# First experts' rows: seven tiles gathered ahead of the last choices, the last tile added by one-hot products

## The chip, the cores and the metric

The kernel runs on one core of one Trainium2 chip. The core has a matrix engine (PE, whose weight loads are shown apart as PEld), three elementwise engines (DVE, ACT, POOL), a queue engine that issues transfers (SP), and 16 DMA engines that every queue shares. The metric is the device time of one execution in microseconds (us). The trace comes from one profiled execution of the kernel; the time is the median of three others.

## The reference, cut to what matters

One layer on 1024 tokens of 1024 channels: a mixer, a residual, a second norm, and a mixture of experts. Only the last two matter here. A router picks one group of 4 and two of 8 experts in it for each token, so each token goes to 2 of 32 experts:

```
x1 = x + gate1 * mixer(...)                       # (1024, 1024)
h  = rmsnorm(x1) * (1 + scale2) + shift2
p_grp = softmax(h @ w_rg + b_rg);  g = argmax(p_grp)
le    = (h @ w_re + b_re)[group g]                # 8 logits
top_p, top_e = top_k(softmax(le), 2);  e = 8 g + top_e
w_tok = p_g * top_p / sum(top_p)
for each expert: rows = h[tokens of the expert]   # here blocks of up to 128 rows
    y = (silu(rows @ w_gate[e]) * (rows @ w_up[e])) @ w_down[e]
x = x1 + gate2 * sum over a token's two experts of w_tok * y
```

Each expert has 6 MB of weights, so that 192 MB are read in the expert stage.

## The kernel before

Tokens are handled in eight tiles of 128. The output projection of the mixer (loop at L1476) makes one tile `t` of `x1` at a time; `residual`, `second_norm` and `router` follow it. `second_norm` (L1169) writes the normed rows to `h2_d` in HBM through POOL's queue; for the last tile (`LT` = 7) the work is cut into halves of 512 channels (`residual`, `scale_half`, `norm_half`, `router_T`, `router` with `hf` 0 and 1), and ACT's queue writes its rows. `choose` (L1227) turns a tile's logits into one-hot choices `oh` and `oab`, a chain of some twenty small DVE instructions.

A token's place among an expert's rows is its rank: matmuls with a strictly triangular matrix of ones (`psr`). Experts 0 and 1 (`FIX` = 2) are always handled first; for them `key` (L1330) holds the place and `sel01` is a one-hot matrix token by place. `first_slots` (L1545) multiplies it with the token numbers in `Vc`, `index` makes an integer of them, and `gather` (L1618) fetches the rows from `h2_d` into `xgs[r]`, cleared beforehand by `clear_xg`. All other experts are ordered by their counts in `order_of_experts` (L1336, three steps divided by `yield`): counts `pst`/`cnt`, a ranking `ord` and `psord`, and the places `pos` of all tokens. `weigh` (L1276) makes the token weights; its first step ends with three exponentials on ACT.

A block of rows goes through `st_x` (eight transposes by PE into `tpx`, split into a high and a low part `tHLx` by an ACT cast and a DVE subtraction, plain copy `tFx`), `st_gu` (products with gate, `wi` 0, and up, `wi` 1), `st_act`, `st_h` and `st_down`. `st_sel` makes the one-hot matrix of a further block, `st_slots` its indices and its gather. The names in the trace end in no number: `tpx` at L1661 is that of blocks 0, 1 and other large ones, at L1677 that of small ones; the third block of the program (number 16) is the first small one.

Weights come in loads of 1 MB into six buffers `big`: two for the gate matrix, two for up, two for down of each expert, in the order of `add_pieces` (L1450). A load is two pieces. `W.split` cuts a piece into a high and a low part (`wh` by ACT, `wl` by DVE, L148), except the up and down pieces of block 0 and all of small blocks, which PE takes whole. A buffer is free when both of its pieces have been split or used, and only then SP, which issues the loads in order, goes on to the load that needs it.

Every engine carries out its own instructions in the order in which the program records them (`tc.manual_schedule`), with waits where one engine needs another's result. PSUM tiles of one bank come from the pool `mps`, which has four buffers:

```
mps = ctx.enter_context(tc.tile_pool(name="mps", bufs=4, space=PSUM))
zps = ctx.enter_context(tc.tile_pool(name="zps", bufs=2, space=PSUM))
e4p = tc.alloc_tile_pool(name="e4p", bufs=3, side="right")
```

`xr` (the input rows of a tile, later its normed rows) and `xg` share the three buffers of `e4p`.

Of the kernel before, what the change touches and what calls it, by code (L numbers as in the profile page):

```python
# [18 lines left out]
P = 128  # L19
# [23 lines left out]
def hybrid_layer_kernel(ctx: ExitStack, tc: tile.TileContext, x, c, w_ada, b_ada, g_norm1, w_in, b_if,  # L43
# [11 lines left out]
    def tt(o, a, b, op, eng=V):  # L55
        return eng.tensor_tensor(out=o, in0=a, in1=b, op=op)  # L56
# [1061 lines left out]
    def k3(ap):  # L1118
        return ap.rearrange("p (k q) -> p k q", q=P)
# [22 lines left out]
    def router(t, hfs=(0, 1)):  # L1142
        for hf in hfs:
            if hf == 0:
                rt[t][1] = mps.tile([P, 512], F32, tag="m", name=f"psl{t}")
            for k in range(4 * hf, 4 * hf + 4):
                mm(rt[t][1][:, 0:36], rt[t][0][:, k, :], wrs[:, k, :], k == 0, k == KT - 1)
        if 1 in hfs:
            stt(logits[:, t, :], rt[t][1][:, 0:36], r2s[t], br, OP.mult, OP.add)
# [74 lines left out]
    def cb(ap, n, m=NT):  # L1224
        return ap.unsqueeze(1).broadcast_to([P, m, n])
# [245 lines left out]
            add_pieces(units[i + 1][0], 1)  # L1471


    xrs[0] = load_xr(0)
    stt(A2, A2, 1.0, g2row, OP.add, OP.mult)
    for t in range(NT):  # L1476
        if t + 1 < NT:
            xrs[t + 1] = load_xr(t + 1)
        mH, mL = mHL[t][:, 0], mHL[t][:, 1]
        if t + 1 < NT:  # L1480
            mg_split(t + 1)
        if 1 <= t < 4:
# [12 lines left out]
        if t < NT - 1:  # L1495
            for k in range(KT):
                products(k, (0, 1))
                if k == 1 and t == NT - 2:
                    drain()
                if k == 2 and t > 0:  # L1500
                    router_T(t - 1)
                if k == 5 and t > 0:
                    router(t - 1)
                    if t == NT - 2:
                        for _ in choose(t - 1, t):
                            pass
            if t == 0:
                router_const()
            if t in (4, 5):
                a_, b_ = ((0, 3), (3, 5))[t - 4]  # L1510
                lat.extend((choose(a_, b_), weigh(a_, b_)))
            for _ in range(6):
                fill(0)
            for hf in range(2):
                residual(t, hf)
            second_norm(t)
        else:
            for k in range(KT):
                products(k, (0,))
                if k == 2:  # L1520
                    router_T(t - 1)
                if k == 5:
                    router(t - 1)
            for _ in choose(t - 1, t):
                pass
            residual(t, 0)
            scale_half(t, 0)
            po[t][1] = zps.tile([P, 2, 512], F32, tag="z", name=f"o{t}_1")[:, 0, :]
            for k in range(KT):
                products(k, (1,))  # L1530
                if k == 4:
                    router_T(t, (0,))
                if k == 6:
                    ranks_early()
                    set_key(slice(0, LT), psr[0][:, 0:LT])
                    S.copy(rank[:, 0:LT], psr[0][:, 0:LT])
            router(t, (0,))
    sel01 = uo.tile([P, FIX, NT, P], BF16, tag="ar", bufs=2, name="sel01")
    psf = {}

    def sel_into(r, sl):
        n = sl.stop - sl.start
        tt(sel01[:, r, sl], cb(iota, P)[:, sl], key[:, sl, r:r + 1].broadcast_to([P, n, P]), OP.is_equal)

    def first_slots(r, a, b):  # L1545
        if a == 0:
            psf[r] = mps.tile([P, 512], F32, tag="m", name=f"slf{r}")
        for t in range(a, b):
            mm(psf[r][:, 0:3], sel01[:, r, t, :], Vc[:, t, 0, 0:3], t == 0, t == NT - 1)

    for r in range(FIX):
        sel_into(r, slice(0, LT))
    yp.release()
    ex = tc.alloc_tile_pool(name="ex", bufs=1, side="left")
    hlR.add(uo, "u", 2, UB, 5)
# [2 lines left out]
    residual(LT, 1)  # L1558
    scale_half(LT, 1)
    mean_square(LT)  # L1560
    router_T(LT, (1,))
    for hf in range(2):
        norm_half(LT, hf)
    router(LT, (1,))
    first_slots(0, 0, LT)
    S.dma_start(h2_d[LT * P:, :], xrs.pop(LT))
# [5 lines left out]
    xgs = [e4(f"xg{i}") for i in range(3)]  # L1572

    def clear_xg(g_):
        S.activation(k3(g_), iota.unsqueeze(1).broadcast_to([P, KT, P]), AF.Copy, scale=0.0)

    for g_ in xgs[0:2]:
        clear_xg(g_)
    for _ in choose(LT, NT):
        pass  # L1580
    mm(psr[1][:, 0:NE], strib, oab[:, LT, :], False, True)
    set_key(slice(LT, NT), psr[1][:, 0:NE].unsqueeze(1))
    S.copy(rank[:, LT, :], psr[1][:, 0:NE])


# [2 lines left out]
    def on_all_rows(o, cols):  # L1588

        for hf in range(2):  # L1590
# [5 lines left out]
    def index(pool, o, ps, c_, name):  # L1596

        sv = pool.tile([P, 1], F32, tag="sv" + name, bufs=6, name=f"sv{name}")
        red(sv, ps[:, c_:c_ + 3], OP.add)
        ts(o, sv, -1.0, OP.add)  # L1600

    def slots(pool, sels, vals, nv, name, c_):

# [75 lines left out]
        return o  # L1679

    ONE = [f"x{b}" for b in WHOLE]
    HALVES = (slice(0, 64), slice(64, 128))

    def st_sel(b):
# [108 lines left out]
            else:  # L1793
                scatter(y, d["idx"])


    for r in range(FIX):
        sel_into(r, slice(LT, NT))
        first_slots(r, LT if r == 0 else 0, NT)
        idx = mo.tile([P, 1], I32, tag="fidx", name=f"fidx{r}")  # L1800
        index(mo, idx, psf[r], 0, f"f{r}")
        gather(xgs[r], idx)
        R[r] = dict(xg=xgs[r])
    def blocks_of(i):
        return units[i] if i < len(units) else []

    places_ = order_of_experts()
# [9 lines left out]
    next(rest)  # L1817
# [6 lines left out]
    W.split()  # L1824
    W.split()
    W.split()
    st_x(1)
    st_sel(0)
    st_gu(0, 1, 0, 4)
    for b in blocks_of(2):  # L1830
        st_slots(b)
    st_slots(0, False)
    if dbg and "key" in dbg:
        nc.sync.dma_start(dbg["key"].rearrange("(t p) n -> p t n", p=P), key)
# [268 lines left out]
```

## Time and profile before

| what | value |
|---|---|
| time, median of 3 (range) | 1400.29 us (1399.58 to 1401.25) |
| the profiled execution's own time | 1400.88 us |
| its span, first to last instruction | 1399.1 us |
| PE busy | 1296.0 us, 93% of the span |
| DVE, ACT, POOL busy | 968.9, 477.7, 230.1 us |
| moved by DMA | 337.50 MB, mean 241 GB/s |

A row of the timeline is read so: start in us from the span's start, duration in us, engine, line, operation, output tile <- input tiles, shape, how many instructions the row merges, and in brackets the idle time before it and what ended it. An f32 product of PE (both operands f32) stands in the trace as two MATMUL instructions, a product of split parts (fp32r) as one. PEclk is the share of full clock that PE was granted: 1.00 is 2.4 GHz, 0.50 is 1.2 GHz.

### The profile page before, as it was taken

The page shows a single profiled execution, that of the slowest core. Times are in us where ns is not written, and L with a number is a line of the kernel's source. Part 1 is how long each engine was busy: PE and PEld are TensorE (multiplying, and loading weights), DVE is VectorE, ACT ScalarE, POOL GpSimd, SP SyncE. Part 2 cuts the span into 40 slices and gives each one's busy share as a digit, 9 for nine tenths or more (in the row PEclk, how much of TensorE's full clock was granted, in tenths as well). Part 3 has the DMA queues.
Part 4 walks back from the last instruction along what each step waited for, and adds up shares of the span by engine and source line. Part 5 has one row for each costly group of instructions (what it writes and reads, how often), then busy time and mean ns, then how long its engine had stood idle before and what let it go on. Part 6 is the DMA issues. An engine that isn't in the chain of part 4 may idle for free. (4 is left out here: it accounts for less than half of the span.)

```text
span 1399.1 us, 17600 instructions
## 1 busy us (share of the span) xinstructions
PE 1296.0 (93%) x6619; PEld 965.0 (69%) x6619; DVE 968.9 (69%) x1402; ACT 477.7 (34%) x650; POOL 230.1 (16%) x230
## 2 busy tenths in 40 slices
PE   3799999999989999899999689999898999999997
PEld 3678998889878888687887555656464756564643
DVE  6969987889997752655547776367575968584636
ACT  5221112223612222621222323225353735353523
POOL 3400111002112220106232002111010211111002
PEclk9799999999999999999999799999999999999999
DMA  9433454323453443455431549899999999999996
GB/s 295 129 121 138 149 181 165 117 80 106 136 158 125 132 144 105 139 166 162 170 118 49 210 184 383 325 379 404 414 411 407 406 380 414 391 409 387 414 385 258
DMA packets 121304, 337.50 MB, mean 241 GB/s; under 512 B 12532, under 2 KB 74272, under 8 KB 96384
## 3 DMA queue, kind: packets, MB, share of 16 engines
q1 hardware_dynamic: 106064, 290.81, 55.7%
q0 software_dynamic: 14672, 43.94, 8.4%
q10 hardware_dynamic: 480, 1.59, 0.3%
q8 instruction: 53, 0.87, 0.2%
q14 instruction: 35, 0.29, 0.1%
HBM read 303.37 MB, written 41.98 MB: 247 GB/s over the span
## 5 line engine op out<-in xcount | busy, mean ns | idle before, releaser
L56 DVE TENSOR_TENSOR wl<-big,wh 128x1024 fp32r<-128x1024 f32 x184 | 224.1, 1255 | 93.3 <-ACT wh L150 92.1
L150 ACT CAST wh<-big 128x1024 fp32r<-128x1024 f32 x184 | 185.6, 1049 | 154.4 <-DMA big<-in_w_e_gate_dram 88.1
L67 PE MATMUL z<-hH,wh 128*128 128x512 f32 x512 | 169.1, 412 | 7.1 <-DVE hH L378 7.1
L67 PE MATMUL gu<-wh,tHLx 128*128 128x512 f32 x528 | 170.7, 404 | 2.1 <-ACT wh L150 1.3
L67 PE MATMUL z<-hL,wh 128*128 128x512 f32 x512 | 163.8, 401 | 0.2 <-POOL hL L56 0.2
L67 PE MATMUL z<-hH,wl 128*128 128x512 f32 x512 | 163.4, 401 | 0.0
L64 DVE SCALAR_TENSOR_TENSOR cacc<-u,vec,cacc 128x1024 f32<-128x1024 f32 x120 | 159.1, 1326 | 2.8
L67 PE MATMUL gu<-big,tFx 128*64 128x512 f32 (+1 forms) x528 | 125.0, 608 | 0.0
L67 PEld LDWEIGHTS z<-hH,wh 128*128 128x128 f32 x512 | 97.6, 195 | 28.8 <-issue 8.1
L67 PEld LDWEIGHTS gu<-wh,tHLx 128*128 128x128 f32 x528 | 97.3, 190 | 28.1 <-ACT wh L150 6.6
L67 PEld LDWEIGHTS z<-hL,wh 128*128 128x128 f32 x512 | 98.5, 192 | 24.9 <-POOL hL L56 0.7
L67 PEld LDWEIGHTS z<-hH,wl 128*128 128x128 f32 x512 | 98.5, 192 | 23.5
L67 PE MATMUL gu<-wl,tHLx 128*128 128x512 f32 x264 | 107.0, 405 | 7.2 <-DVE wl L56 6.9
L1624 POOL DMA_INDIRECT y_d<-ye,idx x24 | 37.7, 1569 | 330.0 <-DVE ye L64 307.3
L67 PEld LDWEIGHTS gu<-big,tFx 128*64 128x64 f32 (+1 forms) x528 | 38.4, 141 | 69.4 <-issue 67.9
L67 PE MATMUL zt<-wh,hH 128*128 128x256 f32 (+1 forms) x256 | 73.1, 286 | 0.0
L67 PE MATMUL o<-woH,mHL 128*128 128x512 f32 x256 | 72.8, 400 | 0.0
L67 PE MATMUL zt<-wh,hL 128*128 128x256 f32 (+1 forms) x256 | 72.8, 284 | 0.0
L67 PE MATMUL zt<-wl,hH 128*128 128x256 f32 (+1 forms) x256 | 72.2, 282 | 0.0
L67 PE MATMUL py<-wh,tHLh 128*128 128x512 f32 x256 | 71.6, 400 | 0.5 <-DVE tHLx L56 0.4
L67 PEld LDWEIGHTS gu<-wl,tHLx 128*128 128x128 f32 x264 | 50.0, 189 | 27.6 <-DVE wl L56 16.9
L56 DVE TENSOR_TENSOR wl<-raw,wh 128x1024 fp32r<-128x1024 f32 (+1 forms) x45 | 57.1, 1274 | 15.7 <-ACT wh L150 15.7
(418 smaller groups left out, 2101.8 us busy)
## 6 DMA issues: line engine op xcount, KB each, us to landing
big<-in_w_e_gate_dram SPq DMA_DIRECT2D x64, 1024.0 KB, 9.8
big<-in_w_e_up_dram SPq DMA_DIRECT2D x64, 1024.0 KB
big<-in_w_e_down_dram SPq DMA_DIRECT2D x64, 1024.0 KB, 8.7
raw<-in_w_in_dram SPq DMA_DIRECT2D x38, 512.0 KB, 4.1
ar<-in_w_ada_dram SPq DMA_DIRECT2D x16, 1024.0 KB, 6.6
araw<-in_w_ada_dram SPq DMA_DIRECT2D x8, 1024.0 KB, 9.6
y_d<-zero SPq DMA_DIRECT2D x16, 512.0 KB, 5.2
xall<-in_x_dram SPq DMA_DIRECT2D x8, 512.0 KB, 8.6
```

The costliest lines, as they stand in the source:

```text
L56: return eng.tensor_tensor(out=o, in0=a, in1=b, op=op)
L64: return V.scalar_tensor_tensor(out=o, in0=a, scalar=s, in1=b, op0=op0, op1=op1)
L67: return PE.matmul(o, l, r, start=start, stop=stop)
L150: S.copy(h, src)
L1624: G.indirect_dma_start(out=y_d[:, :], out_offset=bass.IndirectOffsetOnAxis(ap=idx[:, 1:2], axis=0), in_=src, in_offset=None, bounds_check= ...
```

## The change

Five edits, all around the end of the mixer.

1. The fourth piece of block 0's gate matrix is split in the tile loop, at `t` = 4, into a buffer of the pool `raw`; before, it was split after the last choices.
2. `xg0` and `xg1` are cleared during the last tile; `xg2` only after block 1's transposes.
3. The rows of experts 0 and 1 are gathered with the choices of seven tiles, from `h2_d[0:LT*P]`: both `slf` products and indices stand before the last tile's choices.
4. The last tile's rows come by a product: `sel7[r]` is the one-hot matrix of that tile (f32), `xlast` its normed rows, `last_rows[r]` the product in PSUM, added into `xgs[r]` by DVE (`add_rows`, two halves) when the gather has landed.
5. The work behind it is written in another order: `st_x(0)` before the second step of `order_of_experts`, one quarter of block 0's gate products before it, then the remainder; the first four pieces of block 1's gate are split in two pairs; `add_rows(1)` and `st_x(1)` after the places, two splits, the weights and `st_sel` of the third block; `st_slots` of the third block between the two halves of block 0's up products.

```diff
+    W.pieces[n_dense + 3]["dst"] = lambda: tuple(
+        W.view(wp.tile([P, WB], F32R, tag="raw", bufs=2, name=f"wr{n}"), [P, 2, DE]) for n in "hl")
...
-        if 1 <= t < 4:
+        if 1 <= t < 5:
             W.split()
...
+            xgs.extend(e4(f"xg{i}") for i in range(2))
+            clear_xg(xgs[0])
...
+    for r in range(FIX):
+        psf.append(mps.tile([P, 512], F32, tag="m", name=f"slf{r}"))
+        for t in range(LT):
+            mm(psf[r][:, 0:3], sel01[:, r, t, :], Vc[:, t, 0, 0:3], t == 0, t == LT - 1)
     router_T(LT, (1,))
+    for r in range(FIX):
+        sv = rp.tile([P, 1], F32, name=f"svf{r}")
+        fidx.append(rp.tile([P, 1], I32, name=f"fidx{r}"))
+        red(sv, psf[r][:, 0:3], OP.add)
+        ts(fidx[r], sv, -1.0, OP.add)
+        G.indirect_dma_start(out=xgs[r], out_offset=None, in_=h2_d[0:LT * P, :],
...
+    for r in range(FIX):
+        sel7.append(rp.tile([P, P], F32, name=f"sell{r}"))
+        ts(sel7[r], iota, key[:, LT, r:r + 1], OP.is_equal)
...
+    def add_rows(r):
+        for hf in range(2):
+            tt(xgs[r][:, hf * 512:(hf + 1) * 512], xgs[r][:, hf * 512:(hf + 1) * 512], last_rows[r][:, hf, :], OP.add)
...
+    for r in range(FIX):
+        last_rows.append(zps.tile([P, 2, 512], F32, tag="z", name=f"xl{r}"))
+        for hf in range(2):
+            mm(last_rows[r][:, hf, :], sel7[r], xlast[:, hf * 512:(hf + 1) * 512], True, True)
+    add_rows(0)
     places_ = order_of_experts()
     next(places_)
     rest = weigh(LT - 2, NT)
     next(rest)
     S.activation(mo.tile([P, 1], F32, tag="silu", bufs=1, name="silu"), pio, AF.Silu)
-    W.split()
-    clear_xg(xgs[2])
+    st_x(0)
+    W.nsplit = 4
+    st_gu(0, 0, 0, 1)
     next(places_)
-    st_x(0)
+    st_gu(0, 0, 1, 4)
     next(places_)
...
+    for _ in range(2):
+        W.split()
+    W.prefetch()
     for _ in rest:
         pass
-    W.nsplit = 4
     for b in blocks_of(2):
         st_sel(b)
-    st_gu(0, 0, 0, 4)
...
+    add_rows(1)
     st_x(1)
+    xgs.append(e4("xg2"))
+    clear_xg(xgs[2])
+    st_gu(0, 1, 0, 2)
     for b in blocks_of(2):
         st_slots(b)
...
+    st_sel(0)
+    st_gu(0, 1, 2, 4)
     st_slots(0, False)
```

On PE, at the last tile's router, before (`psl` router products, `x1p` the second half's transposes, `slf` the first experts' token numbers):

```order
L67 MATMUL psl_5855<-wrs,x1T_5820 128x36 x4
L1139 MATMUL x1p_1_5883<-ident,mg 128x128 x4
L67 MATMUL psl_5855<-wrs,x1T_5820 128x36 x4
L67 LDWEIGHTS sel_5860
L67 MATMUL slf_5896<-Vc,sel_5860 128x3
```

and now:

```order
L67 MATMUL psl_5864<-wrs,x1T_5828 128x36 x4
L67 LDWEIGHTS sel_5869
L67 MATMUL slf_5892<-Vc,sel_5869 128x3
...
L67 LDWEIGHTS sel_5869
L67 MATMUL slf_5900<-Vc,sel_5869 128x3
L1139 MATMUL x1p_1_5908<-ident,mg 128x128 x4
L67 MATMUL psl_5864<-wrs,x1T_5828 128x36 x4
L67 LDWEIGHTS strib
L67 MATMUL psr_5842<-oab,strib 128x32
L67 MATMUL xl_5968<-xr_5616,sell_5963 128x512 x2
L67 MATMUL xl_5971<-xr_5616,sell_5965 128x512 x2
```

Both sets of `slf` now stand before the transposes, and four f32 products `xl` stand between the last rank product and the counts `pst`, which follow them.

On PE, from the transposes of block 0 on, `psord` (the ranking of the experts by count) stood before them:

```order
L67 MATMUL psord<-ord_5975,ones 128x32
L67 MATMUL psord<-ord_5976,pio 128x32
L1661 MATMUL tpx_0_6016<-ident,xg_5911 128x128 x4
L1661 MATMUL tpx_1_6024<-ident,xg_5911 128x128 x4
L67 MATMUL gu_6059<-wh_5083,tHLx_6014 128x512 x2
```

and now stands behind the first six products with block 0's gate matrix:

```order
L1665 MATMUL tpx_0_6013<-ident,xg_5740 128x128 x4
L1665 MATMUL tpx_1_6021<-ident,xg_5740 128x128 x4
L67 MATMUL gu_6029<-wh_5083,tHLx_6011 128x512 x2
L67 MATMUL gu_6029<-wl_5084,tHLx_6011 128x512
L67 MATMUL gu_6029<-wh_5083,tHLx_6011 128x512 x2
L67 MATMUL gu_6029<-wl_5084,tHLx_6011 128x512
L67 MATMUL psord<-ord_5987,ones 128x32
L67 MATMUL psord<-ord_5988,pio 128x32
```

All that DVE reads from `psord` now waits for those six products.

On DVE, what stood between the last of the token weights and block 1's `tHLx` before (`sel_6057` is the one-hot matrix of the third block, `wl` a split of a weight piece):

```order
L1314 CAST Vc<-t_4988 128x6
L60 TENSOR_SCALAR pm_6055<-pos 128x16
L56 TENSOR_TENSOR sel_6057<-iota,pm_6055 128x2048
L56 TENSOR_TENSOR wl_6086<-big_5868,wh_6085 128x1024
L56 TENSOR_TENSOR wl_6090<-big_5868,wh_6089 128x1024
L56 TENSOR_TENSOR wl_6094<-big_5869,wh_6093 128x1024
L56 TENSOR_TENSOR tHLx_6097<-tpx_0_6098,tHLx_6097 128x512
```

and now:

```order
L1318 CAST Vc<-t_4988 128x6
L60 TENSOR_SCALAR pm_6096<-pos 128x16
L56 TENSOR_TENSOR sel_6098<-iota,pm_6096 128x2048
L56 TENSOR_TENSOR xg_5741<-xg_5741,xl_5971 128x512 x2
L56 TENSOR_TENSOR tHLx_6102<-tpx_0_6103,tHLx_6102 128x512
L56 TENSOR_TENSOR tHLx_6102<-tpx_1_6110,tHLx_6102 128x512
L1226 TENSOR_REDUCE sv_6141<-sl_6124 128x3
L60 TENSOR_SCALAR idx_6143<-sv_6141 128x2
L56 TENSOR_TENSOR wl_6149<-big_5877,wh_6148 128x1024
L56 TENSOR_TENSOR wl_6153<-big_5877,wh_6152 128x1024
L60 TENSOR_SCALAR pm_6166<-pos 128x16
L56 TENSOR_TENSOR sel_6168<-iota,pm_6166 128x2048
```

The additions into block 1's rows stand behind the third block's one-hot matrix, and PE's transposes of block 1 wait for them; two of the splits have moved up, between `pos` and the token weights.

## Rows read from the trace of the kernel before

**Rows 1.** Windows of four stretches; columns are named in the first row.

```profile
core 0: us, PE busy (x) PEld busy (x) DVE busy (x) ACT busy (x) POOL busy (x), PEclk, DMA share, GB/s
790.00:803.00 13.00, 7.22 (x37) 5.56 (x38) 7.99 (x33) 6.29 (x12) 2.35 (x2) 0.50 0.41 130
826.00:834.00 8.00, 6.33 (x18) 3.88 (x19) 2.79 (x3) 4.94 (x6) 0.00 (x0) 0.79 0.02 8
860.00:930.00 70.00, 67.68 (x348) 40.72 (x345) 33.63 (x40) 21.22 (x28) 7.28 (x6) 1.00 0.88 348
930.00:1300.00 370.00, 348.01 (x1798) 216.97 (x1796) 252.31 (x296) 168.08 (x201) 47.35 (x33) 0.99 1.00 403
```

**Rows 2.** Timeline of PE.

```profile
781.90 0.66 PE L1139 MATMUL x1p<-ident,mg 128*128 128x128 f32 x4 [1.43 <-DVE mg L56]
...
791.30 0.37 PE L67 MATMUL pst<-oab,onesb 128*128 128x32 bf16 x8
...
796.92 1.94 PE L1661 MATMUL tpx<-ident,xg 128*128 128x128 f32 x8 [2.03 <-DMA xg<-h_d,fidx]
...
800.24 0.80 PE L67 MATMUL gu<-wh,tHLx 128*128 128x512 f32 x1 [0.69 <-DVE tHLx L56]
...
807.09 1.06 PE L1661 MATMUL tpx<-ident,xg 128*128 128x128 f32 x8
807.99 7.03 PE L67 MATMUL gu<-big,tFx 128*128 128x512 f32 x16
...
817.55 0.71 PE L67 MATMUL gu<-wh,tHLx 128*128 128x512 f32 x2
...
827.67 1.94 PE L1677 MATMUL tpx<-ident,xg 128*128 128x128 f32 x8 [3.82 <-DMA xg<-h_d,idx]
829.41 7.65 PE L67 MATMUL py<-big,tFh 128*128 128x512 f32 x16
```

**Rows 3.** Timeline of DVE, tile loop and behind it.

```profile
712.23 3.43 DVE L56 TENSOR_TENSOR wl<-big,wh 128x1024 fp32r<-128x1024 f32 x1
...
731.54 0.26 DVE L64 SCALAR_TENSOR_TENSOR logits<-psl,r,br 128x36 f32<-128x36 f32 x1 [5.36 <-PE psl L67]
...
782.83 0.15 DVE L61 TENSOR_SCALAR ss<-ss 128x1 f32<-128x1 f32 x1
...
789.80 0.17 DVE L60 TENSOR_SCALAR key<-key 128x2 f32<-128x2 f32 x1
...
791.74 0.18 DVE L1346 COPY cnt<-pst 128x32 f32<-128x32 f32 x1
...
798.46 0.17 DVE L60 TENSOR_SCALAR elist<-psord 1x32 int32<-1x32 f32 x1
...
799.50 0.68 DVE L56 TENSOR_TENSOR tHLx<-tpx,tHLx 128x512 fp32r<-128x512 f32 x1
...
801.94 0.41 DVE L56 TENSOR_TENSOR kp<-kp,ord 128x256 f32<-128x256 f32 x1
...
807.57 0.17 DVE L60 TENSOR_SCALAR pm<-pos 128x16 f32<-128x16 f32 x1
...
809.98 3.49 DVE L56 TENSOR_TENSOR wl<-big,wh 128x1024 fp32r<-128x1024 f32 x3
```

**Rows 4.** Timeline of ACT.

```profile
786.05 2.00 ACT L1575 ACTIVATE xg<-iota 128x1024 f32<-128x1024 f32 x2 [2.87 <-DVE t L64]
...
794.43 0.21 ACT L1292 ACTIVATE t<-t 128x12 f32<-128x12 f32 x1 [4.45 <-DVE t L56]
...
796.15 0.20 ACT L1811 ACTIVATE silu<-pio 128x1 f32<-128x1 f32 x1
...
798.15 0.56 ACT L150 CAST tHLx<-tpx 128x512 fp32r<-128x512 f32 x1
```

**Rows 5.** Timeline of POOL: the gather of the third block.

```profile
818.10 0.99 POOL L1619 DMA_INDIRECT xg<-h_d,idx  x1 [22.91 <-issue]
```

**Rows 6.** Gathers and loads into tile xg, from issue to landing.

```profile
DMA to landing us min/median/max: 4.2/8.7/11.0
```

More of the change, by code (lines that the diff above doesn't have):

```diff
@@ L1185, in hybrid_layer_kernel, with clear_xg @@
     sq, po = {}, {}
+    xgs, R0 = [], {}
+    def clear_xg(g_):
+        S.activation(k3(g_), iota.unsqueeze(1).broadcast_to([P, KT, P]), AF.Copy, scale=0.0)
     def load_xr(t):
@@ L1536, in hybrid_layer_kernel @@
                     S.copy(rank[:, 0:LT], psr[0][:, 0:LT])
+                    clear_xg(xgs[1])
             router(t, (0,))
     sel01 = uo.tile([P, FIX, NT, P], BF16, tag="ar", bufs=2, name="sel01")
[L1539 to L1549, printed above, removed]
+    psf, fidx = [], []
     for r in range(FIX):
-        sel_into(r, slice(0, LT))
+        tt(sel01[:, r, 0:LT], cb(iota, P)[:, 0:LT], key[:, 0:LT, r:r + 1].broadcast_to([P, LT, P]), OP.is_equal)
     yp.release()
@@ L1560, in hybrid_layer_kernel @@
     mean_square(LT)
+    for r in range(FIX):
+        psf.append(mps.tile([P, 512], F32, tag="m", name=f"slf{r}"))
+        for t in range(LT):
+            mm(psf[r][:, 0:3], sel01[:, r, t, :], Vc[:, t, 0, 0:3], t == 0, t == LT - 1)
     router_T(LT, (1,))
+    for r in range(FIX):
[4 more added lines that the diff above has]
+        G.indirect_dma_start(out=xgs[r], out_offset=None, in_=h2_d[0:LT * P, :],
+                             in_offset=bass.IndirectOffsetOnAxis(ap=fidx[r], axis=0),
+                             bounds_check=LT * P - 1, oob_is_err=False)
     for hf in range(2):
@@ L1564, in hybrid_layer_kernel @@
     router(LT, (1,))
-    first_slots(0, 0, LT)
-    S.dma_start(h2_d[LT * P:, :], xrs.pop(LT))
+    xlast = xrs.pop(LT)
+    S.dma_start(h2_d[LT * P:, :], xlast)
     wp2.release()
@@ L1571, in hybrid_layer_kernel @@
     S.dma_start(gt2, mod_r[3:4, :].broadcast_to([P, D]))
[L1572 to L1578, printed above, removed]
     for _ in choose(LT, NT):
@@ L1582, in hybrid_layer_kernel @@
     set_key(slice(LT, NT), psr[1][:, 0:NE].unsqueeze(1))
+    sel7 = []
+    for r in range(FIX):
+        sel7.append(rp.tile([P, P], F32, name=f"sell{r}"))
+        ts(sel7[r], iota, key[:, LT, r:r + 1], OP.is_equal)
+        R0[r] = dict(xg=xgs[r])
     S.copy(rank[:, LT, :], psr[1][:, 0:NE])
@@ L1594, in on_all_rows @@
             S.copy(o[:, hf * 512:(hf + 1) * 512], ps)
[L1596 to L1600, printed above, removed]
     def slots(pool, sels, vals, nv, name, c_):
@@ L1681, in hybrid_layer_kernel @@
     ONE = [f"x{b}" for b in WHOLE]
+    last_rows = []
+    def add_rows(r):
+        for hf in range(2):
+            tt(xgs[r][:, hf * 512:(hf + 1) * 512], xgs[r][:, hf * 512:(hf + 1) * 512], last_rows[r][:, hf, :], OP.add)
     HALVES = (slice(0, 64), slice(64, 128))
@@ L1794, in st_down @@
                 scatter(y, d["idx"])
[L1797 to L1803, printed above, removed]
     def blocks_of(i):
         return units[i] if i < len(units) else []
+    R.update(R0)
+    for r in range(FIX):
[3 more added lines that the diff above has]
+    add_rows(0)
     places_ = order_of_experts()
@@ L1811, in hybrid_layer_kernel @@
     S.activation(mo.tile([P, 1], F32, tag="silu", bufs=1, name="silu"), pio, AF.Silu)
-    W.split()
-    clear_xg(xgs[2])
+    st_x(0)
+    W.nsplit = 4
+    st_gu(0, 0, 0, 1)
     next(places_)
-    st_x(0)
+    st_gu(0, 0, 1, 4)
     next(places_)
-    next(rest)
+    for _ in range(2):
+        W.split()
+    W.prefetch()
     for _ in rest:
         pass
-    W.nsplit = 4
     for b in blocks_of(2):
         st_sel(b)
-    st_gu(0, 0, 0, 4)
-    W.split()
-    W.split()
-    W.split()
+    add_rows(1)
     st_x(1)
-    st_sel(0)
-    st_gu(0, 1, 0, 4)
+    xgs.append(e4("xg2"))
+    clear_xg(xgs[2])
+    st_gu(0, 1, 0, 2)
     for b in blocks_of(2):
         st_slots(b)
+    for _ in range(2):
+        W.split()
+    W.prefetch()
+    st_sel(0)
+    st_gu(0, 1, 2, 4)
     st_slots(0, False)
```

## The prediction

> **What bounds the kernel now.** I read the windows first, to see what sets the pace behind the changed place. From 930 to 1300 us the DMA share is 1.00 and the rate 403 GB/s, while PE is busy 348.01 of 370 us; from 860 to 930 us it is PE that is nearly full (67.68 of 70 us, DMA 0.88) [rows 1]. So the expert stage is a stream of weights with a matrix engine close behind it. It starts late: from 826 to 834 us the DMA share is 0.02 [rows 1]. Nothing was in flight; the next weights were waiting for a buffer, and the buffers for work of the first blocks. So what counts is when that work gets done. I take as its mark the products `py` of block 0, which free the down buffers, at 829.41 us [rows 2]. Loads and blocks after that hang on it, so whatever delays it delays the end.
>
> Then I followed PE back from there. The transposes of the third block began at 827.67 us, after 3.82 us of waiting for its gather [rows 2], which POOL issued at 818.10 us [rows 5]. Its indices stand on PE behind block 0's up products, and these behind block 1's transposes at 807.09 us, for which PE did not wait [rows 2]. Block 0's transposes at 796.92 us had waited 2.03 us for their gather [rows 2]; that is the wait that the change takes out. But the cast behind them came only at 798.15 us, since ACT first did the exponentials (794.43), a table load and silu (796.15) [rows 4]. PE's clock was 0.50 from 790 to 803 us [rows 1].
>
> **The change part by part.** The sum is made against the profiled execution (1400.88 us, span 1399.1), 0.59 us above the median of 1400.29; the difference is carried over to the median.
>
> *The fourth split, sooner.* In the tile loop a split beside POOL's addition takes DVE 3.43 us; before the logits of a tile DVE idled 5.36 us [rows 3]. It is hidden there, at 0; without that cover it would cost up to 3.43. It saves one split behind the choices (a third of 3.49, 1.16 us, on DVE [rows 3]) and lets one load each of up and down go earlier. On SP the up load passes one load of input rows; its split is done before that would be issued, so 0. The loads themselves gain nothing: all had landed by 826 us [rows 1].
>
> *The clears.* Two of 1.0 us each [rows 4] go into ACT's idle time in the last tile. The first stands ahead of a copy for the router: 0 to 1.0 us, taken at 0, since ACT has few other tasks there.
>
> *The transposes of the last router.* `slf` for two experts now stands before them, and `mps` has four banks. At that point the rank tile `psr1`, the router's `psl` and two `slf` hold all four. The transposes need one back, which the reduction of the first `slf` on DVE gives. It stands behind the mean square `ss`, at 782.83 plus 0.15, and takes about as long: 783.2 against 781.90 us [rows 2, 3], so +1.3. The four transposes then run wholly at half clock: eight took 1.94 us there and 1.06 at full [rows 2], so up to 0.44 more for four. I take +1.6 (bounds 1.3 and 1.8). The whole chain of choices shifts by it: `key` is ready at 789.97 + 1.6 = 791.6.
>
> *The products `xl`.* A one-hot matrix on DVE is not in the trace; between the smallest instruction (0.15) and a 128x512 one (0.68) [rows 3] I take 0.25. Eight f32 products of 512 columns took 7.03 us at full clock [rows 2], 0.88 each; at half clock 1.76. Four cost 3.5 us at full clock and 7.0 at half. The clock is low here (0.50, which is 1.2 GHz), and may rise on the way, as it did between 796.92 and 807.09 us, where the same eight transposes took 1.94 and 1.06 [rows 2]; I take half clock for the first two and about 2.4 for the others, 5.9, done at 797.75 us. Then `pst` (0.37 [rows 2]): `cnt` at 798.1, against 791.74 [rows 3], +6.4 (4.0 to 7.6). DVE's additions for block 0 (two of 0.68) fit beside the last two products. The gather, issued about 1 us behind its index (783.4), is in by 795.4 even at the 11.0 us maximum [rows 6].
>
> *To the first products.* From `cnt` to the exponentials 2.69 us, and from these until silu is nearly done (796.25) 1.82 [rows 3, 4]: the cast of block 0 at 802.6. It was 798.15; 1.9 us of a cast and a clear that stood in between are gone, so +4.5. DVE's low part follows at once, 803.25 against 799.50 [rows 3]: +3.75. PE's second product starts at 804.0, not 800.24 [rows 2]. So the wait that was removed comes back larger, on ACT.
>
> *`psord` and DVE's row.* `psord` waits behind six products, five of them after 804.0. From 800.24 to 807.09 us 23 of them took 0.30 us each in the mean, part of it at half clock [rows 2]; between that and twice that I take 0.43 each, 2.15, plus `psord` itself, four short f32 instructions at the price of four transposes (0.95): `elist` on DVE at 807.1 against 798.46 [rows 3]. From there DVE has, before it adds block 1's rows: 1.04 (798.46 to 799.50), places and token weights 5.63 (801.94 to 807.57), the third block's matrix 2.41 (807.57 to 809.98), two splits 2.33 (two thirds of 3.49) and the additions, 2 x 0.68 [rows 3]. That is 12.8 us: 819.9. PE, done with block 0's gate at 804.0 + 6.85 (as from 800.24 to 807.09) + about 0.6 = 811.4, waits 8.5 us. Block 1's transposes move from 807.09 to 819.9, +12.8; none of that wait was there before.
>
> *To the third block.* After 3.82 us of idling eight transposes took 1.94 us [rows 2], so after 8.5 PE is at half clock too: transposes 1.8 us, and half of the up products 5.1 (3.5 at full, 7.0 at half), to 826.8. Then indices and gather, issued some 1.8 us later as PE, DVE and POOL hand on: 828.6 against 818.10 [rows 5]. It lands after 8.7 us, the median, at 837.3 (4.2 to 11.0: 832.8 to 839.6) [rows 6]. Meanwhile DVE, from 827.9, makes two splits and block 0's matrix (2.33 + 2.41), and PE the sixteen small slot products, some 0.5 (`pst`'s eight took 0.37 [rows 2]): block 1's gate starts at 833.0, not 817.55 [rows 2]. To its end it takes 6.3 us (817.55 to 823.85, where the wait of 3.82 began [rows 2]): 839.2. The gather is then no longer waited for. So the third block's transposes start +11.5, not +15.5: the old wait takes back 3.82.
>
> *Clock.* PE now comes there without a pause. Before, from 827.67 to the end of `py` it took 9.4 us [rows 2]; at full clock 1.06 + 7.03 less the overlap, 8.0. So -1.4.
>
> The sum is 11.5 - 1.4 = +10.1 us at `py`, and I take +10.0. Nothing behind it is faster or slower, and the next loads start with `py`, so it goes to the end: 1410.3 us on the scale of the median.
>
> The row for the wait removed is 2.03 us [rows 2]. The Trainium skill (DMA: Bandwidth & Descriptors, Rules for kernel authors) says to issue a DMA early, compute, and wait for it late, so that its fixed cost overlaps. By that alone the sum would be -2.0, a rival below; the rows on ACT and DVE say that other waits end later.
>
> **The rivals.** *Only the gather's wait goes* (faster). Block 0 starts 2.0 us sooner and hands this on through the third block's gather: 1398.3. It decides if DVE has added block 1's rows before PE ends block 0's gate (811.4 in my reckoning). For it: the 2.03 us were real, and PE had no wait at 807.09. Against it: 12.8 us of DVE work in a fixed order stand before those additions.
>
> *Half given back later.* If two loads of 1 MB more than before had landed when `py` starts, the stream would be 2 x 2.6 us (1 MB at 403 GB/s) ahead and 4.8 remain: 1405.1. For it: one down and one up load do go sooner. Against: the load that follows needs the down buffer that `py` frees, in both kernels.
>
> *All given back.* If PE's 22 us of idling between 930 and 1300 us [rows 1] were slack against something that does not shift, the end would stay: 1400.3. Against: the DMA is full there, and shifts too.
>
> *The gathers are not early.* If POOL's wait for the rows of the seventh tile or the full queues held the first gather until after 798 us, the change would not do what it says, and 1 to 3 us come on top: 1412.3. The median of 8.7 us speaks against it.
>
> **How the numbers follow.** The forecast has 0.78, half given back 0.10, all given back 0.05, gathers late 0.03, only the wait 0.04. The forecast's own range comes from its unknown terms: `xl` at full clock -2.4, the clock high again soon after the long wait -1.9, a low clock throughout +2.5, the gather at 11.0 us +0.4, the router's transposes -0.3 to +0.2, the first clear up to +1.0. Not all fall together: +5.5 to +13.5, so 1405.8 to 1413.8. With the rival of half the loss the range is 1404.5 to 1414.0. A measurement of this kernel tells 0.2%, 2.8 us, from no change; so faster 0.04, same 0.05, slower 0.91.
>
> **What would show it.** In the changed kernel: `x1p`'s second four about 1.3 us later behind a DVE reduction; `cnt` near 798; the cast of block 0 waiting on the exponentials, not on the gather; a PE wait of 6 to 10 us before block 1's transposes, ended by DVE's addition into `xg`; no wait before the third block's; `py` of block 0 near 839.5; the DMA idle until about 843; and the same stream after that, shifted. I am wrong if block 1's transposes start before 812 us, or if `py` is late and the end is not.

## The result: slower by 0.8%, as forecast, and the profile after

The changed kernel took 1413.74 us in the median of 4 runs (1411.13 to 1414.46), the kernel before, run beside it, 1400.77 (4 runs, 1399.58 to 1404.45). The ratio is 1.0080, 95% interval 1.0052 to 1.0108: 11.2 us more, between 7.3 and 15.1. The two medians themselves stand 13.0 us apart, so the size is known only within that interval. The forecast was 1410.3 us, +10.0: that increase lies inside the interval, while the median of 1413.74 stands just under the upper end of the forecast's range (1404.5 to 1414.0). The profiled execution of the changed kernel took 1411.13 us (span 1409.4), 10.25 us more than the profiled one of before (1400.88).

First PE's timeline of the changed kernel, which answers to [rows 2]; columns are start, duration, engine, line, operation, tiles, size and count, in brackets the idle time before and what ended it.

```profile
782.70 1.12 PE L1139 MATMUL x1p<-ident,mg 128*128 128x128 f32 x4 [1.47 <-DVE svf L1226]
...
791.61 5.95 PE L67 MATMUL xl<-xr,sell 128*128 128x512 f32 x8 [0.78 <-DVE sell L60]
...
797.60 1.14 PE L1665 MATMUL tpx<-ident,xg 128*128 128x128 f32 x8
803.02 1.52 PE L67 MATMUL gu<-wh,tHLx 128*128 128x512 f32 x2 [4.29 <-ACT tHLx L150]
...
819.65 1.97 PE L1665 MATMUL tpx<-ident,xg 128*128 128x128 f32 x8 [8.35 <-DVE xg L56]
821.41 4.63 PE L67 MATMUL gu<-big,tFx 128*128 128x512 f32 x8
...
831.57 0.56 PE L67 MATMUL sl<-Vc,sel 128*128 128x9 bf16 x16 [1.61 <-DVE sel L56]
...
838.14 1.06 PE L1681 MATMUL tpx<-ident,xg 128*128 128x128 f32 x8
839.04 7.03 PE L67 MATMUL py<-big,tFh 128*128 128x512 f32 x16
845.90 0.95 PE L67 MATMUL sl<-Vc,sel 128*128 128x9 bf16 x32
```

The wait that the change was to remove has a longer one in its place: PE waits 4.29 us for ACT's cast where block 0's gather was waited for 2.03. A new wait comes with it, 8.35 us for DVE's addition where PE had none. The last wait of before (3.82, for the third block's gather) is gone: that gather landed 5.2 us after its issue at 827.75, about 5 us before PE came to it. `py` starts at 839.04, 9.63 later than in [rows 2].

DVE and ACT, which answer to [rows 3, 4], one fence each:

```profile
795.43 1.28 DVE L56 TENSOR_TENSOR xg<-xg,xl 128x512 f32<-128x512 f32 x2 [3.68 <-PE xl L67]
797.79 0.19 DVE L1350 COPY cnt<-pst 128x32 f32<-128x32 f32 x1 [1.07 <-PE pst L67]
...
803.00 0.69 DVE L56 TENSOR_TENSOR tHLx<-tpx,tHLx 128x512 fp32r<-128x512 f32 x1 [2.31 <-ACT tHLx L150]
...
806.94 0.18 DVE L60 TENSOR_SCALAR elist<-psord 1x32 int32<-1x32 f32 x1 [1.42 <-PE psord L67]
...
816.10 2.29 DVE L56 TENSOR_TENSOR sel<-iota,pm 128x2048 bf16<-128x2048 f32 x1
818.31 1.28 DVE L56 TENSOR_TENSOR xg<-xg,xl 128x512 f32<-128x512 f32 x2
```

```profile
800.56 0.21 ACT L1296 ACTIVATE t<-t 128x12 f32<-128x12 f32 x1 [9.32 <-DVE t L56]
...
801.00 1.28 ACT L1818 ACT_TABLE_LOAD   x1
802.29 0.20 ACT L1818 ACTIVATE silu<-pio 128x1 f32<-128x1 f32 x1
802.40 0.57 ACT L150 CAST tHLx<-tpx 128x512 fp32r<-128x512 f32 x1
```

PE's transposes were done at 798.7; ACT, idle for 9.32 us until DVE had the inputs of the exponentials, cast only at 802.40. On DVE, 12.7 us lie between `elist` and the end of the additions for block 1.

POOL has the gathers (the first line serves as the zero of the table below), and the windows answer to [rows 1]:

```profile
782.67 0.56 POOL L146 TENSOR_TENSOR r<-ss,mhalf 128x1 f32<-128x1 f32 x1 [10.68 <-DVE svf L1226]
783.71 1.32 POOL L1571 DMA_INDIRECT xg<-h_d,fidx  x1 [0.48 <-issue]
...
827.75 1.08 POOL L1623 DMA_INDIRECT xg<-h_d,idx  x1 [41.41 <-issue]
```

```profile
790.00:803.00 13.00, 7.32 (x25) 3.55 (x24) 5.20 (x24) 2.56 (x7) 0.00 (x0) 0.76 0.13 51
803.00:826.00 23.00, 14.63 (x49) 9.45 (x50) 14.73 (x40) 7.56 (x10) 0.00 (x0) 0.70 0.14 47
...
834.00:846.00 12.00, 12.00 (x49) 7.36 (x48) 8.15 (x7) 5.44 (x7) 0.00 (x0) 1.00 0.46 164
...
930.00:1300.00 370.00, 349.44 (x1798) 217.46 (x1797) 256.75 (x301) 169.99 (x202) 49.61 (x35) 0.99 0.99 400
```

PE is busy 14.6 of 23 us from 803 to 826. Far behind it the stream is as full as before, and only later.

**One scale for all traces.** Where the tile loop ends differs by several us from execution to execution, whatever the kernel. The loop itself does not: from POOL's square root of its first tile to that of its last it takes 101.23 to 101.36 us in both kernels. So marks are counted from POOL's square root for the last tile (`r<-ss`, 782.67 here; 783.08 in the first trace of before, 785.43 in a second one). The last column is the ratio to the kernel before, in per mille above or below, with its interval; the experiments of one group below ran on one chip with their own runs of before.

| kernel | cnt | cast | elist | block 1 | gather 3 | py | behind py | ratio, ‰ |
|---|---|---|---|---|---|---|---|---|
| before | 8.7 | 15.1 | 15.4 | 24.0 | 35.0 | 46.3 | 53.8 | |
| before, second trace | 8.7 | 15.1 | 15.4 | 24.0 | 35.0 | 44.2 | 52.7 | −0.1 (−1.9 to 1.7) |
| after | 15.1 | 19.7 | 24.3 | 37.0 | 45.1 | 56.4 | 63.2 | 8.0 (5.2 to 10.8) |
| after, second trace | 15.2 | 19.8 | 24.4 | 37.1 | 45.2 | 56.5 | 63.3 | 6.9 (4.2 to 9.7) |
| 1 additions early | 14.8 | 19.5 | 24.3 | 31.1 | 38.2 | 51.0 | 57.8 | 2.6 (0.4 to 4.8) |
| 2 counts first | 9.0 | 15.1 | 18.5 | 31.2 | 40.2 | 51.5 | 58.3 | 4.3 (2.6 to 6.0) |
| 3 no xl | 9.0 | 13.6 | 18.5 | 25.0 | 32.3 | 45.2 | 52.0 | −0.2 (−2.3 to 1.9) |
| 4 new order | 7.4 | 13.7 | 12.0 | 24.0 | 30.2 | 41.4 | 48.3 | −2.6 (−4.5 to −0.7) |
| 7 new order, DVE too | 7.4 | 16.7 | 12.4 | 23.5 | 30.6 | 39.6 | 46.5 | −3.2 (−5.2 to −1.3) |
| 8 fourth split alone | 8.7 | 15.1 | 15.4 | 24.0 | 35.0 | 44.0 | 52.6 | 0.5 (−1.2 to 2.3) |
| 9 up halved alone | 8.7 | 15.2 | 15.5 | 25.5 | 32.8 | 44.2 | 52.6 | −2.0 (−4.1 to 0.1) |
| 10 order alone | 8.7 | 15.3 | 15.6 | 25.5 | 31.5 | 41.2 | 48.0 | −3.0 (−5.1 to −1.0) |
| 11 as 7 | 7.4 | 16.7 | 12.4 | 23.5 | 30.6 | 39.6 | 46.5 | −3.3 (−5.3 to −1.3) |
| 12 x1p not waiting | 14.2 | 18.8 | 23.6 | 36.3 | 44.4 | 55.7 | 62.6 | 7.4 (5.3 to 9.5) |

"py" is the start of block 0's down products; "block 1" and "gather 3" are the start of block 1's transposes and the issue of the third block's gather; "behind py" is the start of the slot products `sl` that follow `py`. Two traces of one kernel agree to 0.1 us at every mark up to the gather, so these can be compared to tenths, where whole times can't. One limit holds for marks behind the cast: they also hang on the clock that PE was granted. In experiments 9 and 10 block 1 comes at 25.5, not 24.0, with PE's code ahead of it as in the kernel before; over block 0's gate products PEclk was 0.61 and 0.62 there, and 0.73 in the three traces (before, second trace of before, experiment 8) that have 24.0.

### The profile page after: what moved, and what is told of

The parts are those of the page before. It is cut to its first block, busy times and chain, and to the rows that moved or that the text cites. A ratio compares the mean times of both kernels' runs of the same rounds, so it can differ in the third digit from the quotient of the medians.

```text
span 1409.4 us, 17619 instructions
## 1 busy us (share of the span) xinstructions
PE 1302.5 (92%) x6625; PEld 969.9 (69%) x6625; DVE 973.7 (69%) x1406; ACT 477.6 (34%) x650; POOL 229.9 (16%) x230
## 5 line engine op out<-in xcount | busy, mean ns | idle before, releaser
L67 PEld LDWEIGHTS gu<-wh,tHLx 128*128 128x128 f32 x524 | 96.2, 189 | 30.6 <-ACT wh L150 5.9
L56 DVE TENSOR_TENSOR wl<-raw,wh 128x1024 fp32r<-128x1024 f32 (+1 forms) x45 | 57.1, 1273 | 15.5 <-ACT wh L150 15.5
L67 PEld LDWEIGHTS gu<-wl,tHLx 128*128 128x128 f32 x262 | 49.5, 189 | 26.3 <-DVE wl L56 15.6
```

The source lines that it names most:

```text
L67: return PE.matmul(o, l, r, start=start, stop=stop)
```

## The experiments

All start from the changed kernel unless said otherwise.

### 1 to 4: what the loss is made of

*1.* One line moved:

```
     next(rest)
+    add_rows(1)
...
-    add_rows(1)          # behind places, weights, st_sel and two splits
     st_x(1)
```

> The changed kernel with one line moved: the additions of the last tile's rows for block 1 stand on DVE right behind the inputs of the exponentials, no longer behind 12.6 us of places, weights, selection matrix and splits. Theory (DVE's order is the largest single term, but not the whole): block 1's transposes start at about 811 us instead of 819.65, without a wait for DVE's addition; then the third block's selection matrix on the same DVE is late next (done near 817), its gather is issued near 820 instead of 827.75, and block 0's down products come at about 835 instead of 839.0: 4 us less, 1407 on the scale of the profiled run (1411.1). Rival A (that wait is the whole loss): 9 us less, 1402. Rival B (the loss is PE's, from the f32 products, and the wait before block 1 only stands where PE would wait anyway): within 1 us of the changed kernel.

PE's timeline of it:

```profile
810.13 1.05 PE L1665 MATMUL tpx<-ident,xg 128*128 128x128 f32 x8
811.02 3.60 PE L67 MATMUL gu<-big,tFx 128*128 128x512 f32 x8
814.82 0.56 PE L67 MATMUL sl<-Vc,sel 128*128 128x9 bf16 x16 [0.21 <-DVE sel L56]
815.24 3.68 PE L67 MATMUL gu<-big,tFx 128*128 128x512 f32 x8
820.98 0.56 PE L67 MATMUL sl<-Vc,sel 128*128 128x9 bf16 x16 [2.06 <-DVE sel L56]
```

The 8.35 us of waiting are gone, and `py` is 5.4 us sooner, behind `py` as well. That is nearer the theory (4) than rivals A (9) and B (1). DVE's selection matrices are waited for next, though not quite as the theory said: the third block's for 0.21 us only, block 0's, which it did not name, for 2.06. Block 1 came at 31.1 on the common scale, which is 813.8 on that of the changed kernel and not 811: block 0's gate products were granted 0.55 of full clock here, 0.79 in the changed kernel. The ratio, 2.6 ‰, is 6.0 us below that of the second run of the changed kernel, on another chip.

*2.* Only the order of emission in front of the first block:

```
+    places_ = order_of_experts(); next(places_)
     (four xl products)
+    rest = weigh(LT - 2, NT); next(rest)
     add_rows(0)
-    places_ = order_of_experts(); next(places_)
-    rest = weigh(LT - 2, NT); next(rest)
```

> The changed kernel with the counts of the experts (the products pst and DVE's chain behind them) and the inputs of the exponentials ahead of the f32 products xl; nothing else moves. Theory (xl delays everything behind the choices by 6 us at cnt, of which most is hidden again behind later waits of DVE): cnt at 792 instead of 797.8, the cast of block 0 at 798.5 to 799.5 instead of 802.4, elist at 804, block 1's transposes about 817; block 0's down products 1.5 to 2.5 us earlier, total about 1409.3. Rival (the 6 us of xl pass one for one to the end): 1405.

`cnt` came 6.1 us sooner and `py` 4.9: more than twice the theory's 2 and nearer to the rival (ratio 4.3 ‰, 6.0 us above before). Its PE timeline shows what the theory had missed:

```profile
787.56 5.67 PE L67 MATMUL xl<-xr,sell 128*128 128x512 f32 x8 [0.56 <-DVE sell L60]
793.07 1.06 PE L1665 MATMUL tpx<-ident,xg 128*128 128x128 f32 x8
794.35 0.50 PE L67 MATMUL gu<-wh,tHLx 128*128 128x512 f32 x1 [0.22 <-ACT tHLx L150]
...
801.05 0.39 PE L67 MATMUL gu<-wrl,tHLx 128*128 128x512 f32 x1
809.80 1.97 PE L1665 MATMUL tpx<-ident,xg 128*128 128x128 f32 x8 [8.35 <-DVE xg L56]
```

With the exponentials done during `xl`, PE waits 0.22 us for the cast, not 4.29. PE thus comes to block 0's gate with hardly a pause, and its products were granted 1.00 of full clock, against 0.79 in the changed kernel; `psord` stands behind six fast products, and `elist` gains 5.8 us. From `elist` to block 1 it takes 12.71 us in both kernels (12.68 in experiment 12): that is DVE's row. PE's wait of 8.35 us in it is the same to the hundredth because PE's products behind `psord` are fast in both (a pair in 0.63 us, most of them); in experiment 12, where the first of them take 1.05 to 1.22 us a pair, the wait is 6.98.

*3.* The four `xl` products and the additions are left out.

> The changed kernel without the products xl and without the additions (it leaves out the last tile's rows of the first two blocks), so that only the early gathers, the clears and the early split are left of the change. Theory (products and additions, with DVE's order, cost all that was lost; the wait removed was worth little): cnt at 792, the cast of block 0 at about 797 because the exponentials and the table load stand ahead of it on ACT, block 1's transposes at 805 to 806, block 0's down products at 826 to 827 against 829.4 before the change: 1398 to 1399, so 2 to 3 us under the kernel before. Rival (early gathers or the router's wait for a bank cost too): 1402 or more. Rival (the removed wait is worth more than 2 us): under 1396.

`py` is 11.2 us sooner than in the changed kernel and within 1.2 us of the two traces of before; the ratio is 0.9998. So products and additions, with what waited for them, cost all of the loss. What is left of the change comes out even as a whole: the early gathers, the router's wait for a bank (`key` at 8.39, as in the changed kernel) and also the order of edit 5, which this kernel keeps although the expectation does not list it. The other half of the theory is not borne out: the mark behind `py` is 0.7 and 1.8 us sooner than in the two traces of before, not 2 to 3, and the interval of the ratio (−3.2 to 2.7 us) can't tell. PE and ACT of this run:

```profile
793.43 1.95 PE L1665 MATMUL tpx<-ident,xg 128*128 128x128 f32 x8 [0.18 <-DMA xg<-h_d,fidx]
799.10 1.52 PE L67 MATMUL gu<-wh,tHLx 128*128 128x512 f32 x2 [3.72 <-ACT tHLx L150]
...
809.65 0.40 PE L67 MATMUL gu<-wrl,tHLx 128*128 128x512 f32 x1
```

```profile
797.08 1.28 ACT L1813 ACT_TABLE_LOAD   x1
798.37 0.20 ACT L1813 ACTIVATE silu<-pio 128x1 f32<-128x1 f32 x1
798.48 0.57 ACT L150 CAST tHLx<-tpx 128x512 fp32r<-128x512 f32 x1
```

Block 0's transposes start 8.6 us behind the square root, 5.1 sooner than in the second trace of before (799.13 − 785.43 = 13.7). The gathers were issued 8.3 us sooner, but each took 7.4 to 8.4 us to land, against 4.3 to 4.8 there. The cast behind them comes 1.5 us sooner (13.6 to 15.1), because it stands behind the table load and `silu`. PE then waits 3.72 us, and from the gate's first product to its last takes 10.55 us (799.10 to 809.65) where experiment 2 took 6.70 (794.35 to 801.05); over the gate's products PEclk was 0.57, against 1.00 there. The Trainium skill (DMA: Bandwidth & Descriptors, Rules for kernel authors) has a DMA issued early and waited for late. The trace agrees as far as the transposes (0.18 us of waiting where the second trace of before has 2.00), and no further.

*4.* The same early gathers and `xl` in another order:

```
     next(places_); next(rest); silu      # counts and exponentials first
     xl of block 0; add_rows(0)
     next(places_)                        # psord, elist
     xl of block 1
     next(places_); st_x(0); st_gu(0, 0, 0, 4)
     add_rows(1)                          # ahead of the splits
```

and the second `slf` behind `router_T(LT, (1,))`.

> The change with another order: counts and the inputs of the exponentials first, xl of block 0, then psord, then xl of block 1; on DVE the additions of block 0, the places, and the additions of block 1 ahead of the splits; and the second slf behind the router's transposes, so that these need not wait for a bank. Theory (the loss is one of order, not of the early gathers): elist at about 795 instead of 806.9, no wait for DVE before block 1's transposes (807), the third block's gather issued near 814, block 0's down products near 825 against 829.4 before the change: 1397, 3 to 4 us under the kernel before and 14 under the changed one. Rival (xl's 6 us on PE can't be hidden): 1401 to 1404.

```profile
805.99 1.06 PE L1668 MATMUL tpx<-ident,xg 128*128 128x128 f32 x8
...
823.48 7.03 PE L67 MATMUL py<-big,tFh 128*128 128x512 f32 x16
```

`elist` came at 12.0, block 1 at 24.0 without a wait, the gather at 30.2, `py` at 41.4: on the scale of the changed kernel's trace 794.7, 806.6, 812.8 and 824.1, where the theory had 795, 807, 814 and 825. The ratio is −2.6 ‰, 3.7 us under the kernel before. The same products `xl` and the same additions stand in this kernel, so the loss was one of order. The rival (6 us of `xl` can't be hidden) falls.

### 5 to 8: the same kernels again, and single parts

*5 and 6.* The kernels before and after, unchanged.

> The kernel before, unchanged, to have a trace of it on the chip of these runs and a measure of what two sets of one kernel differ by. Theory (what follows block 0's down products is the same stream in every kernel, and only this chip makes it longer): ratio 1.000 within 0.002, and from py to the end 574 to 575 us as in the four earlier experiments, not the 569.7 of the first trace of it. Rival (the early experiments lost 4 to 5 us behind py, because their stream started sooner but went no faster): 570 us here.

> The changed kernel, unchanged, beside the kernel before on this chip. Theory (10.0 us at py go to the end one for one): ratio 1.0055 to 1.0085, 8 to 12 us above the kernel before; py 56.4 us behind POOL's square root of the last tile (46.3 before). Rival (a further loss of 3 us that the one profiled run missed): 13 us or more, 1.0092 and above.

Both theories hold (ratios 0.9999 and 1.0069, which is 9.7 us; from `py` to the end the kernel before took 575.6 us here, a little more than the 574 to 575 foretold). The second trace of before (PE's timeline) also shows that the first was not typical in one place:

```profile
799.13 1.94 PE L1661 MATMUL tpx<-ident,xg 128*128 128x128 f32 x8 [2.00 <-DMA xg<-h_d,fidx]
...
828.58 1.25 PE L1677 MATMUL tpx<-ident,xg 128*128 128x128 f32 x8 [2.35 <-DMA xg<-h_d,idx]
829.63 8.65 PE L67 MATMUL py<-big,tFh 128*128 128x512 f32 x16
```

The third block's gather was waited for 2.35 us here (2.26 in experiment 8), against 3.82 in [rows 2]. `py` starts sooner but then takes 8.65 us, at 0.81 of full clock in the mean. So the better mark is the end of `py`: there the loss is 63.2 − 53.8 = 9.4 us by the first pair of traces and 10.6 by the second.

*7.* Experiment 4, with weights and the third block's matrix ahead of two splits, and `st_sel(0)` ahead of the next two.

> The order of the fourth experiment, with two more moves on DVE alone: weights and the third block's selection matrix ahead of two splits, and block 0's selection matrix ahead of the next two. Theory (with the waits of the change gone, DVE's order in front of the slot products is the bound): the third block's gather 0.5 us sooner, block 0's slot products no longer waited for, py 1.5 to 2.5 us sooner than in the fourth experiment, 39 to 40 us behind POOL's square root against 46.3 before the change; ratio 0.994 to 0.997. Rival (PE's order is the bound, DVE's rows have slack): py at 41.4, ratio 0.9974 as there.

PE's timeline:

```profile
812.46 0.55 PE L67 MATMUL sl<-Vc,sel 128*128 128x9 bf16 x16
812.86 3.68 PE L67 MATMUL gu<-big,tFx 128*128 128x512 f32 x8
816.71 0.56 PE L67 MATMUL sl<-Vc,sel 128*128 128x9 bf16 x16 [0.17 <-DVE sel L56]
```

The wait for block 0's matrix fell from 1.61 us in experiment 4 to 0.17, and `py` came at 39.6, 1.8 sooner. The gather came 0.4 later, not 0.5 sooner: in this run `xl` took 3.78 us for each block, at half clock, and the cast was at 16.7. Ratio −3.2 ‰; the two orders can't be told apart by time.

*8.* The kernel before with the fourth split alone.

> The kernel before with the fourth split in the tile loop as the only part of the change. Theory (its 3.4 us on DVE lie beside DVE's waiting in the tile loop, and the load and the split saved later are off the path): POOL's square root of the last tile and py within 0.5 us of the kernel before, ratio 0.999 to 1.001. Rival A (a split less in DVE's row behind the choices is worth its 1.2 us): py 1.2 us sooner. Rival B (cover gone): tile loop up to 3.4 us longer.

All marks are those of the second trace of before, so rival A falls; the ratio is 0.5 ‰ (−1.2 to 2.3). The tile loop takes 101.30 us from its first square root to its last, against 101.36 and 101.27 in the two traces of before, so rival B falls too. The split is hidden, and wins nothing by itself.

### 9 to 12: does the new order need the early gathers?

*9.* The kernel before; only block 0's up products in halves:

```
-    st_sel(0); st_gu(0, 1, 0, 4)
-    st_slots(third block)
+    st_gu(0, 1, 0, 2)
+    st_slots(third block)
+    st_sel(0); st_gu(0, 1, 2, 4)
```

> The kernel before with one part of the change alone: block 0's up products in two halves, the slot products of the third block between them, and block 0's selection matrix behind these. No early gather, no xl. Theory (the one part of the change that helps is this one): the third block's gather 2.4 us sooner (35.0 to 32.6 us behind POOL's square root), PE's wait before its transposes (3.82, 2.35 and 2.26 us in three traces without it) gone or nearly, py 1.5 to 2.5 us sooner, 42 to 42.7 against 44.2; ratio 0.998 to 0.9995. Rival (block 0's selection matrix, now later, takes all of it back at PE): py at 44.

The rival's number came, `py` at 44.2 as in the second trace of before, but not by its way: PE waits only 0.53 us for block 0's selection matrix (1.79 in the second trace of before). The gather is issued 2.3 us sooner, yet it took 10.2 us to land (8.0 there), so PE still waited 1.93 us for it:

```profile
818.08 0.56 PE L67 MATMUL sl<-Vc,sel 128*128 128x9 bf16 x16 [0.53 <-DVE sel L56]
...
826.73 1.30 PE L1677 MATMUL tpx<-ident,xg 128*128 128x128 f32 x8 [1.93 <-DMA xg<-h_d,idx]
```

Block 1 also started 1.5 us later, behind gate products at the lower clock (0.61 of full clock, against 0.73); with that made up for, the theory's 1.5 us might have shown. The ratio, −2.0 ‰ (−4.1 to 0.1), decides nothing.

*10 and 11.* The kernel before with these halves and two of the three splits behind `st_sel(0)`; and experiment 7 again beside it.

> As the ninth, and two of the three splits before block 1's transposes put behind block 0's selection matrix. Still no early gather and no xl. Theory (the gain of the seventh experiment over the kernel before is one of order on DVE, and the early gathers add nothing to it): the third block's gather at about 30.3 us behind POOL's square root, block 1's gate not waiting for block 0's slot products, py at 39.5 to 40.5, as in the seventh (39.6); ratio 0.9955 to 0.998. Rival (early gathers carry that gain): py at 42 or later, ratio 0.9985 or more.

> The kernel of the seventh experiment again, beside the tenth on one chip. Theory (early gathers neither gain nor lose once the order is right): the two within 0.002 of each other, both 0.995 to 0.998 of the kernel before. Rival: this one lower by 0.002 or more.

PE of experiment 10:

```profile
805.91 1.05 PE L1661 MATMUL tpx<-ident,xg 128*128 128x128 f32 x8
...
810.23 0.55 PE L67 MATMUL sl<-Vc,sel 128*128 128x9 bf16 x16
810.64 3.68 PE L67 MATMUL gu<-big,tFx 128*128 128x512 f32 x8
814.15 0.55 PE L67 MATMUL sl<-Vc,sel 128*128 128x9 bf16 x16
...
820.71 1.06 PE L1677 MATMUL tpx<-ident,xg 128*128 128x128 f32 x8
821.60 7.03 PE L67 MATMUL py<-big,tFh 128*128 128x512 f32 x16
```

No wait is left from block 1's transposes to `py`, although gathers and choices stand as in the kernel before. `py` at 41.2 is a little later than forecast, since block 1 starts at 25.5. The ratios are −3.0 and −3.3 ‰ (medians 1398.57 and 1398.70 us): the theory holds, the two are the same within what can be measured. Both beat both kernels. The gain comes from the order of splits, selection matrices and slot products. The 1.6 us at `py` between the two can't be put down to the early gathers: experiment 11 has block 1 at 23.5, 2.0 sooner, and from there to `py` it takes 16.1 us, experiment 10 only 15.7.

*12.* The second `slf` behind the router's transposes.

> The changed kernel with the slot products of block 1 behind the router's last transposes, so that these find a bank free without DVE's reduction. Theory (the term of 1.6 us is a shift of the whole chain): the second four transposes at -1.1 us instead of 0.0 behind POOL's square root, cnt 1.6 us sooner (13.5 instead of 15.1), and all marks up to py sooner by 1.2 to 1.6 us (py about 55); total 1.5 us less than the changed kernel, 1.005 to 1.008 of the kernel before. Rival (a later wait hides it): cnt sooner, py unchanged at 56.4.

The transposes came 1.1 us sooner, `key` 1.26 (7.13 behind the square root, against 8.39 after and 6.72 before), `cnt` 0.96 and `py` 0.66. So there is a shift, but at `py` it is half of the theory's 1.2 to 1.6, between theory and rival: `xl` takes 6.26 us here instead of 5.95 and gives some back. In the time (7.4 ‰) it can't be seen.

## Why the prediction was right

**The frame.** That the stream starts with `py` of block 0 and that a delay there goes to the end, one for one, held. From the slot products behind `py` to the end it took 562.2 us before and 563.5 after, and 567.1 and 565.5 in the second pair; over all traces that stretch ranges from 562.2 to 568.6, so single executions show it only to a few us. Experiments 1, 2 and 3 moved that mark by −5.4, −4.9 and −11.2 us, and the ratios by −4.3, −2.6 and −7.1 ‰ (6.0, 3.6 and 10.0 us) against the second run of the changed kernel. The rivals of half or all given back (4.8 us or nothing left, 3.4 or 0 ‰) lie outside both intervals of the changed kernel (5.2 to 10.8 and 4.2 to 9.7 ‰).

**The terms.** On the scale of the profile the changed kernel's tile loop ended 0.4 us sooner than that of before, so each foretold time is a few tenths late.
- The gathers were early: the first is issued at 783.71 us. The fourth split at 0: experiment 8.
- The transposes of the last router: +1.6 foretold at `key`, +1.67 measured. Undoing their wait returns 1.26 of it.
- `xl` at 5.9 us: 5.95 (6.02 in the second trace), at 0.61 of full clock. That the clock would rise midway was a guess: in the other experiments the same four products took 5.4 to 7.6 us. `cnt` at 798.1: 797.79.
- The cast at 802.6, behind the exponentials: 802.40.
- `elist` at 807.1: 806.94. 12.8 us of DVE's row before PE can go on: 12.7; block 1 at 819.9: 819.65, after 8.35 us of waiting (8.5).
- Half of the up products 5.1 us: 4.63. The gather at 828.6: 827.75. Block 1's gate at 833.0: 831.98.
- The third block at 839.2: 838.14, not waiting for its gather. The clock at −1.4: from those transposes to the slot products behind `py` 7.76 us, 9.22 before, −1.46. The DMA engines then stand idle until 843.6 us (about 843 foretold).

**What was off, and where luck helped.** The sum adds up to the end of `py` (it counts the clock within `py`), but the forecast sets its +10.0 at the start (839.5). On the common scale the start moved by 10.0 us in the first pair of traces and by 12.2 in the second, the end by 9.4 and 10.6. The term "the old wait takes back 3.82" came from one execution; other traces show 2.35 and 2.26. It was in part compensated: in those `py` took longer (8.65 and 8.73 us against 7.65). So +10.0 at the start of `py` is in part the luck of the one trace; at the end it holds in both. The gather was assumed to land after 8.7 us; it took 5.2, off the path. And the rival "only the gather's wait goes" was given 2.0 us; experiment 3 shows that even with `xl` at no cost its removal wins at most 1.8 us behind `py` and nothing that the time shows, in this order, since ACT's table load holds the cast and PE's clock the gate.

**Shown and not shown.** Shown by experiments: `xl` and the additions, where they stand, are the whole loss; moving the additions returns 5.4 us, moving the counts 4.9, and with both moved nothing of it is left. Not shown: what the early gathers are worth by themselves, since in experiment 3 they come with edit 5's order, and between experiments 10 and 11 the clock over block 0's gate differs too (0.62 and 1.00). Why kernels with the same code ahead of that gate get different clocks there stays open.

## What to carry to other kernels

A wait that is removed at the head of a chain is worth only what the next wait on each engine leaves: look for the cast behind a table load and the addition behind a row of small operations before counting it. When an early transfer has to be paid for with work at the latest moment, put that work behind the counts and tables that everything else hangs on, and write the additions where DVE waits anyway. And try the new order without the new idea: here it gave the same 3 ‰.

## What the runs showed of the hardware

- The same four f32 products `xl` took 5.4 us in experiment 4 (3.40 + 1.99) and 7.6 in experiment 7 (3.78 twice): over these products PEclk was 0.75 in the one and 0.50 in the other (0.50 again when that kernel ran a second time). PE had the same instructions before them, and in the 10 us before was busy for 3.35 and 3.38 us; the traces do not show why the clock differed.
- The third block's gather landed after 9.4, 8.0 and 7.9 us in three traces with the kernel before's code for it, 10.2 in experiment 9 and 5.2 in the changed kernel. The load on the DMA engines does not tell which: while the gather was in flight the DMA share was 0.79, 0.91 and 0.86 in the first three, 0.97 in experiment 9 and 0.93 in the changed kernel. The gathers of blocks 0 and 1 took 4.2 to 5.5 us in two traces of before, with the DMA share at 0.27 and 0.31, and 7.6 to 8.7 us in the changed kernel, 8.4 us sooner, at 0.86.
- Whole times of the kernel before ranged from 1395.61 to 1410.94 us on one chip, while marks within the changed stage agreed to 0.1 us between two traces of one kernel: a trace settled what 12 timed runs could not, as long as the granted clock was the same.
